# Two-layer diffusion backbone on one core: a matrix cast by its transfer, a later 1/rms, and a new order of the last FFN's operand sums

## The chip, the core and the metric

The kernel runs on one core of a Trainium2 chip. The metric is device time in microseconds. A core has engines that each work through their own queue in order: TensorE (PE) for matmuls, VectorE (DVE), ScalarE (ACT), GpSimd (POOL) and SyncE (SP). SP and POOL mostly start transfers (DMA). An instruction that waits holds up everything behind it on its engine.

## The reference

The reference is a hybrid backbone with two layers over 1024 latent tokens of width 1024 and 256 context tokens.

```
layer 0:  p = u @ w_in;  y = [2-D Fourier mix | order-2 Hyena (short conv, two long convs by FFT)] @ w_out
layer 1:  neighbourhood attention (16 heads, relative bias, all context keys) @ w_out
each:     u = rms_norm(h, norm_g) * (1 + scale) + shift        # scale and shift from the conditioning vector
          h = h + g1 * mixer(u)
          h = h + g2 * ((silu(u2 @ w_gate) * (u2 @ w_up)) @ w_down)
out:      rms_norm(h_lat, final_g)
```

Here `rms_norm(x, g) = x * rsqrt(mean(x * x) + 1e-6) * g`. The FFN has 2816 hidden channels. In layer 1 only the latent tokens go on to the output projection and the FFN.

## The kernel before

Activations are held channel by token: a tile has 128 channels on the partitions and 512 tokens in the free dimension. `pc` 0 and 1 are the two halves of the latent tokens, `pc` 2 the context. Each float32 product is made of three matmuls: an operand is split into a rounded high part (a cast on ACT) and the low part that is left (a subtraction on DVE). `split` at L285 does this for weights and activations (L287 is the cast, L289 the subtraction); `out` in `wino_second` does the same at L1172 and L1173. So an operand is ready only when ACT and then DVE have worked on it. Weights come through `weights` (L307): a float32 load into a `ws` buffer by SP, then the split into `wh` and `wl`. These three tags have two buffers each.

A scheduler decides at build time in which order the instructions stand in each engine's queue. `self.follow(x)` (L226) makes it place what is issued inside behind the instruction x. The generators in the source (their `yield`s are the steps) say what is issued in which order; the scheduler may move instructions where dependences allow.

**First forward transforms (layer 0).** `in_proj` (L744) multiplies 16 blocks of the input projection and feeds `short_conv` (L727; ACT L737, then DVE L738 to L741). Then `hy_forward("l", 0)` (L791) transposes the folded channels on TensorE (L802), splits them (L287, L289), and multiplies them with the matrices `vf_l`. Each matrix comes as float16: `cmat` (L321) loads it through SP into a `cs` tile of the tag `ws` and ACT casts it (L335) into a `mat` tile of the tag `wh` or `wl`. Another helper, `cast` (L338), already used elsewhere for the matrices `ff_l`, starts a transfer on POOL's queue that converts on the way and writes the `mat` tile directly; it goes round the tags `wh`, `wl`, `ws`.

**Last output projection (layer 1).** `first_part(1)` (L2040) multiplies the first six of eight channel blocks of the second token half with `w_out2`: eight blocks of output channels, 18 matmuls each, with a yield behind each three. Behind each block `add_h` (L2030) adds to the residual h2. The loop at L2075 weaves in the RMS norm of the first token half. `square` (L470) has squared its eight blocks on ACT (L475) into tiles of the pool `tk`, which has four buffers, and added them on DVE (L480). At step 2 `rms_begin(0)` (L482) adds over the channels with four matmuls of one column and takes square root and reciprocal (L493, L495). At step 5 `rms_end` (L498) spreads 1/rms over the partitions: four scalings of the identity on ACT (L504) and one matmul. From there `wino_first` (L1148) makes the FFN's operands of the first half, one step at each third step. The attention's last output rows are stored from `tk` tiles as well (`d<-tk` on POOL's queue).

**Last FFN (layer 1).** `ffn` multiplies by a seven-product Winograd scheme over 2 x 2 blocks (token halves by channel halves). `wino_steps` (L1264) orders the products: A11*B11, A12*B21, S1*T1, S2*T2, S3*T3, A22*T4, S4*B22, each over four 128-row pieces j = 0 to 3, for gate and up. The S operands come from weights, the T operands from activations: `wino_second` (L1163) makes T1 (four times: `scaled(j)`, a subtraction, `out`), then T2 (`scaled(j + 4)` at L1179, a sum at L1195, `out`), then T3 (sum at L1200, `out`), T4 (sum at L1206, `out`) and B22. `scaled` multiplies a block of the second half by its norm and modulation. In layer 1 the `scaled(j + 4)` of T2 follow the last subtraction of T1; the sums of T3 and T4 are free to move. `snap` (L1277) copies an accumulator from PSUM on ACT (L1279) before the next product is added to it.

Of the kernel before, what the change touches and what calls it, by code (L numbers as in the profile page):

```python
# [10 lines left out]
F32 = mybir.dt.float32  # L11
# [5 lines left out]
MUL, ADD, SUB, MAX, MIN = ALU.mult, ALU.add, ALU.subtract, ALU.max, ALU.min  # L17

P = 128
# [181 lines left out]
class Builder:  # L201
# [40 lines left out]
    def T(self, dt=F32, w=512):  # L242
        self.tk = (getattr(self, "tk", 0) + 1) % 8
        if self.tk >= 6 and self.banks == 8 and not hasattr(self, "od"):
            return self.TK(dt, w)
        return self.pt.tile([P, w], dt, tag="t", name=self.nm("t"))
# [4 lines left out]
    def PS(self):  # L251
        self.pk = (self.pk + 1) % self.banks
        return self.PQ() if self.pk >= 6 else self.pp.tile([P, 512], F32, tag="ps", name=self.nm("ps"))
# [244 lines left out]
    def rms_end(self, pc, c, copy=True):  # L498

        nc = self.nc  # L500
        w = WID[pc]
        t = self.T()
        for j in range(w // P):
            nc.scalar.mul(t[:, j * P:(j + 1) * P], self.ident, c[:, j:j + 1])  # L504
        ps = self.PS() if self.banks == 8 else self.PQ()
        self.mm(ps[:, :w], self.ones, t[:, :w], True, True)
        if copy:
            nc.scalar.copy(t[:, :w], ps[:, :w])
            return t
        return ps  # L510
# [280 lines left out]
    def hy_forward(self, sq, o):  # L791
        nc, a = self.nc, self.a
        PS, T = (self.PS, self.T) if sq == "l" else (self.PQ, self.T)
        nb = 4 if sq == "l" else 1
        H = nb * P
        ab = self.ab[sq]
        tr = {}
        for b in range(nb):
            for s in (0, 1):
                ps = PS()  # L800
                for cb in range(4):
                    nc.tensor.transpose(ps[:, cb * P:(cb + 1) * P], ab[cb][:, s * H + b * P:s * H + (b + 1) * P],  # L802
                                        self.ident)
                hi, lo = self.S2(F32R), self.S2(F32R)
                self.split(ps, hi, lo)
                tr[(s, b)] = (hi, lo)
        yield
        Y = self.Y[(sq, o)] = {}
        for cls in (0, 1):
            for fb in range(nb):  # L810
                spec = []
                for i, s in ((cls, cls), (2 + cls, 1 - cls)):
                    mt = self.cmat(2 * H, a["vf_" + sq][i, fb], None, False)
                    mh, ml = mt[:, :H], mt[:, H:]
                    ps = PS()
                    for b in range(nb):
                        sl = slice(b * P, (b + 1) * P)
                        xh, xl = tr[(s, b)]
                        self.mm(ps, mh[:, sl], xh, b == 0, False)
                        self.mm(ps, mh[:, sl], xl, False, False)  # L820
                        self.mm(ps, ml[:, sl], xh, False, b == nb - 1)
                    spec.append(ps)
                d = self.frg[(sq, o, cls, fb)]
                fr, g = self.TK(), self.TK()
                self.ld(fr, d[0])
                self.ld(g, d[1])
                fr2 = fr
                if cls == 0 and fb == 0:
                    fr2 = self.S2()
                    self.ld(fr2, d[2])  # L830
                c, s = spec
                for kind, (x0, x1, op) in enumerate((((c, fr), (s, g), SUB), ((c, g), (s, fr2), ADD))):
                    t0, t1 = T(), T()
                    nc.vector.tensor_tensor(t0, x0[0], x0[1], MUL)
                    nc.vector.tensor_tensor(t1, x1[0], x1[1], MUL)
                    nc.gpsimd.tensor_tensor(t0, t0, t1, op)
                    if nb == 4:
                        key = (kind, cls, fb // 2)
                        if key not in Y:
                            Y[key] = (self.S4(F32R), self.S4(F32R))  # L840
                        hi, lo = (q[:, (fb % 2) * 512:(fb % 2) * 512 + 512] for q in Y[key])
                    else:
                        hi, lo = self.S2(F32R), self.S2(F32R)
                        Y[(kind, cls, 0)] = (hi, lo)
                    self.split(t0, hi, lo)
                yield
# [316 lines left out]
    def wino_second(self, h, l, m, r):  # L1163

        nc = self.nc
        dsh = self.C(4)
        ad = self.ada[(l, 0)]
        nc.vector.tensor_tensor(dsh, ad[:, m * 8 + 4:m * 8 + 8], ad[:, m * 8:m * 8 + 4], SUB)

        def out(key, j, src):  # L1170
            hi, lo = self.pair((key, j), l == 1 or len(self.X) < 17)
            nc.scalar.copy(hi, src)  # L1172
            nc.vector.tensor_tensor(lo, src, hi.bitcast(F32), SUB)  # L1173

        ts, sub = [], None

        def scaled(b):
            t = h.ap(0, b, 1)
            nc.vector.scalar_tensor_tensor(t, t, self.ada_col(l, 1, m + 1, b), r, op0=MUL, op1=MUL)  # L1179
            return t  # L1180

        for j in range(4):
            t11, t21 = self.raw.pop(j), self.raw.pop(j + 4)
            with self.follow(sub if l else None):
                t12 = scaled(j)
            sub = nc.vector.tensor_tensor(t11, t12, t11, SUB).ins
            out("T1", j, t11)
            ts.append([t11, t12, None, t21])
            yield
        for j in range(4):  # L1190
            with self.follow(sub if l else None):
                ts[j][2] = t22 = scaled(j + 4)
            t11 = ts[j][0]
            sh = self.ada_col(l, 1, m, j + 4)
            nc.vector.scalar_tensor_tensor(t11, t22, sh, t11, op0=ADD, op1=SUB)  # L1195
            out("T2", j, t11)
            yield
        for j in range(4):
            t11, t12, t22, t21 = ts[j]
            nc.vector.scalar_tensor_tensor(t12, t22, dsh[:, j:j + 1], t12, op0=ADD, op1=SUB)  # L1200
            out("T3", j, t12)
            yield
        for j in range(4):
            t11, t12, t22, t21 = ts[j]
            sh = self.ada_col(l, 1, m, j + 4)
            nc.vector.scalar_tensor_tensor(t21, t21, sh, t11, op0=ADD, op1=SUB)  # L1206
            out("T4", j, t21)
            yield
        for j in range(4):
            t22 = ts[j][2]  # L1210
            sh = self.ada_col(l, 1, m, j + 4)
            hi, lo = self.pair(("B22", j), l == 0 and len(self.X) < 17)
            nc.scalar.activation(hi, t22, AF.Identity, bias=sh)
            nc.vector.scalar_tensor_tensor(lo, t22, sh, hi.bitcast(F32), op0=ADD, op1=SUB)
            yield
# [604 lines left out]
    def run(self):  # L1820
        nc, a = self.nc, self.a
# [195 lines left out]
        h2, o, h4 = Act(), Act(), Act()  # L2017
# [21 lines left out]

        def first_part(pc):  # L2040
            for nb in range(KB):
                wh, wl = self.weights(a["w_out2"][nb, :, :768], 768, load=None if pc else self.ldr)
                acc = self.PQ() if pc == 0 else self.PS()
                for kb in range(6):
                    if pc == 0 and nb == 0:
                        load_o(kb, (0,), self.ld)
                        yield 1
                    if pc == 0 and nb == 2:
                        load_o(kb, (1,), self.ld)
                    if kb == 2:  # L2050
                        if pc or nb == 0:
                            load_h2(nb, pc)
                        if pc == 0 and nb < 7:
                            load_h2(nb + 1, pc)
                    for w, part in ((wh, 0), (wh, 1), (wl, 0)):
                        self.mm(acc, w[:, kb * P:(kb + 1) * P], by_row(o.ap(part, kb, pc)),
                                kb == 0 and w is wh and part == 0, kb == 5 and w is wl)
                    yield 0.5
                add_h(nb, pc, acc)
# [15 lines left out]
        for i, _ in enumerate(first_part(1)):  # L2075
            if i == 2:
                c = self.rms_begin(0)
            if i == 5:
                first = self.wino_first(h2, 1, 3, self.rms_end(0, c))
            if i > 5 and i % 3 == 1:  # L2080
                next(first, None)
        sums = {}
        drain(self.wino_pair(1, 0, 0, sums, self.G))
# [31 lines left out]
        c = self.rms_begin(1)  # L2115
# [85 lines left out]
```

## Time and profile before

| | us |
|---|---|
| median of three runs | 3024.45 (3024.08 to 3025.89) |
| profiled execution, its time | 3021.79 |
| profiled execution, its span | 3020.0 |
| TensorE busy | 2894.4 |
| DVE busy | 2079.7 |
| ACT busy | 1363.0 |
| POOL busy | 478.9 |

The span runs from the first to the last instruction of the profiled execution. A row of a timeline gives the start, the busy time, the engine, the line of the source, the operation, output and inputs by the program's names, and the number of instructions that the row joins; in brackets stands how long the engine was idle before and what ended that. In a table of stretches each engine has its busy time and instructions (in parentheses), and behind them stand the clock granted to TensorE as a share of full speed, the busy share of the DMA engines and the GB/s moved.

### The profile page before, as it was taken

The numbers are of one execution on the slowest core, as the hardware profiler recorded it, in microseconds if no ns is written. First come the engines' busy times: TensorE is split into PE (matmuls) and PEld (weight loads), VectorE is DVE, ScalarE is ACT, GpSimd is POOL, SyncE is SP. The second block draws the span as 40 slices with busy tenths as digits, with TensorE's granted clock in tenths as the row PEclk, the third lists the DMA queues.
The fourth block names the chain that finished last, engine by engine and source line by source line (L and its number), as shares of the span: only waits on it lengthen the run. The fifth ranks groups of instructions, "written<-read, shape, count | busy, mean of one in ns | idle before, by whom it ended". The sixth has DMA issues, their size and how long they took to land. (4 is left out here: it accounts for less than half of the span.)

```text
span 3020.0 us, 45776 instructions
## 1 busy us (share of the span) xinstructions
PE 2894.4 (96%) x16320; PEld 2414.6 (80%) x16320; DVE 2079.7 (69%) x3988; ACT 1363.0 (45%) x2549; POOL 478.9 (16%) x785
## 2 busy tenths in 40 slices
PE   7899999999999999999999999999899999999997
PEld 2678888888899788788888888878777788888886
DVE  5677786675677777876777437777677977665454
ACT  3453325453455333333445337777675533333442
POOL 1112013452100111112020000110111022112000
PEclk9899999999999999999999999999999999999998
DMA  8764545456555554659884344444555266435663
GB/s 279 247 222 168 178 146 172 122 181 230 189 183 196 174 185 170 213 186 324 318 291 155 126 129 118 129 139 124 177 184 203 89 235 216 175 113 184 212 194 119
DMA packets 263486, 558.26 MB, mean 185 GB/s; under 512 B 33878, under 2 KB 85784, under 8 KB 263258
## 3 DMA queue, kind: packets, MB, share of 16 engines
q1 hardware_dynamic: 205050, 372.84, 37.8%
q0 software_dynamic: 55904, 178.30, 16.5%
q10 hardware_dynamic: 2304, 4.20, 0.4%
q8 instruction: 128, 2.10, 0.3%
q14 instruction: 100, 0.82, 0.1%
HBM read 418.63 MB, written 119.80 MB: 178 GB/s over the span
## 5 line engine op out<-in xcount | busy, mean ns | idle before, releaser
L1274 PE MATMUL ps<-s,s 128*128 128x512 f32 x2028 | 505.9, 391 | 12.8 <-ACT g L1279 4.6
L1274 PEld LDWEIGHTS ps<-s,s 128*128 128x128 f32 x2028 | 380.9, 188 | 97.2 <-ACT g L1279 7.1
L283 PE MATMUL ps<-s,wh 128*128 128x256 f32 (+1 forms) x1768 | 393.4, 328 | 2.3 <-DVE s L720 1.2
L283 PEld LDWEIGHTS ps<-s,wh 128*128 128x128 f32 x1768 | 292.7, 189 | 38.1 <-ACT wh L287 2.5
L283 PE MATMUL pq<-s,wh 128*128 128x512 f32 (+1 forms) x984 | 299.4, 383 | 0.6 <-DVE s L1658 0.6
L287 ACT CAST wh<-ws 128x1024 fp32r<-128x1024 f32 (+1 forms) x139 | 142.4, 1024 | 334.7 <-PE ps L283 158.4
L1445 PE MATMUL ps<-s,s 128*128 128x512 f32 (+1 forms) x1000 | 258.4, 383 | 4.5 <-DVE s L289 4.4
L289 DVE TENSOR_TENSOR wl<-ws,wh 128x1024 fp32r<-128x1024 f32 (+1 forms) x139 | 165.3, 1190 | 136.0 <-ACT wh L287 134.2
L283 PE MATMUL ps<-s,wl 128*128 128x256 f32 (+1 forms) x884 | 255.8, 326 | 1.2 <-DVE wl L289 1.2
L287 ACT CAST s<-s 128x1024 fp32r<-128x1024 f32 (+2 forms) x184 | 168.2, 940 | 187.9 <-DMA s<-d 169.6
L283 PE MATMUL ps<-s,s 128*128 128x64 f16 (+3 forms) x2663 | 217.0, 233 | 24.3 <-DVE st L1743 10.3
L287 ACT CAST s<-t 128x512 fp32r<-128x512 f32 (+2 forms) x250 | 139.7, 579 | 182.2 <-DVE t L1253 68.4
L289 DVE TENSOR_TENSOR s<-s,s 128x1024 fp32r<-128x1024 f32 (+2 forms) x162 | 186.8, 1184 | 46.9 <-ACT s L287 46.4
L1445 PEld LDWEIGHTS ps<-s,s 128*128 128x128 f32 x1000 | 184.4, 188 | 42.9 <-DVE s L289 6.7
L289 DVE TENSOR_TENSOR s<-t,s 128x512 fp32r<-128x512 f32 (+2 forms) x250 | 166.9, 680 | 57.8 <-ACT s L287 31.2
L283 PEld LDWEIGHTS pq<-s,wh 128*128 128x128 f32 x984 | 177.7, 190 | 34.2 <-DVE s L1658 2.1
L1274 PE MATMUL ps<-s,wh 128*128 128x512 f32 x608 | 193.3, 395 | 0.3 <-DVE g L1367 0.3
L283 PE MATMUL ps<-s,mat 128*128 128x512 f32 x684 | 178.5, 408 | 4.9 <-ACT s L287 4.0
L283 PE MATMUL pq<-s,wl 128*128 128x512 f32 (+1 forms) x492 | 182.1, 380 | 0.0
L283 PEld LDWEIGHTS ps<-s,wl 128*128 128x128 f32 x884 | 162.6, 188 | 18.4 <-DVE wl L289 1.9
L283 PEld LDWEIGHTS ps<-s,mat 128*128 128x128 f32 x684 | 132.3, 196 | 39.8 <-ACT s L287 6.2
L1445 PE MATMUL ps<-s 128*128 128x512 f32 (+1 forms) x500 | 149.4, 385 | 0.0
(381 smaller groups left out, 5621.8 us busy)
## 6 DMA issues: line engine op xcount, KB each, us to landing
s<-d SPq DMA_DIRECT2D x282, 256.0 KB, 3.6
s<-in_down SPq DMA_DIRECT2D x150, 256.0 KB, 4.0
d<-s POOLq DMA_DIRECT2D x137, 256.0 KB, 3.6
d<-tk POOLq DMA_DIRECT2D x98, 256.0 KB, 3.6
s<-in_ada_w POOLq DMA_DIRECT2D x48, 512.0 KB, 4.7
g<-in_bias SPq DMA_DIRECT2D x128, 192.0 KB, 2.8
ws<-in_up SPq DMA_DIRECT2D x44, 512.0 KB, 3.4
d<-g POOLq DMA_DIRECT2D x87, 256.0 KB, 3.1
```

The lines of the kernel that those rows point to most:

```text
L283: self.nc.tensor.matmul(o, l, r, start=st, stop=sp)
L287: self.last_hi = nc.scalar.copy(hi, src).ins
L289: self.last_lo = eng.tensor_tensor(lo, src, hi.bitcast(F32), SUB).ins
L1274: nc.tensor.matmul(ps, x[:, sl], y, start=first and j == 0 and x is wh and y is xh, stop=j == 3 and x is wl, skip_group_check=True)
L1445: m = nc.tensor.matmul(acc[j][:, c0:c1], x[:, sl], y[:, xs], start=first and k == 0, stop=last and k == 2, skip_group_check=True)
```

## The change

There are three edits.

1. The first four `vf_l` matrices of the first forward transform (`cls` 0, `fb` 0 and 1, two each) are fetched with `cast` instead of `cmat`.
2. `rms_end(0)` and `wino_first` are issued at step 11 of `first_part(1)` instead of step 5, and `wino_first` advances from step 13 on. The loads and splits of that projection's weights for blocks 3 to 8 (`nb` over 1) follow the last scaling of the most recent `rms_end`, which is the one of step 11 for those blocks.
3. In layer 1, `wino_second` notes every low-part subtraction of `out`. The scalings `scaled(j + 4)` follow the third one (T1, j = 2), the sums of T3 follow the seventh (T2, j = 2), and the sums of T4 follow the eleventh (T3, j = 2). The scalings no longer follow the last subtraction of T1.

```
@@ rms_end
-            nc.scalar.mul(t[:, j * P:(j + 1) * P], self.ident, c[:, j:j + 1])
+            self.last_mul = nc.scalar.mul(t[:, j * P:(j + 1) * P], self.ident, c[:, j:j + 1]).ins
@@ hy_forward
-                    mt = self.cmat(2 * H, a["vf_" + sq][i, fb], None, False)
+                    src = a["vf_" + sq][i, fb]
+                    mt = self.cast(2 * H, src) if sq == "l" and o + cls == 0 and fb < 2 else self.cmat(2 * H, src)
@@ wino_second
-            nc.vector.tensor_tensor(lo, src, hi.bitcast(F32), SUB)
+            los.append(nc.vector.tensor_tensor(lo, src, hi.bitcast(F32), SUB).ins)
+
+        los = []
+
+        def behind(n):
+
+            return self.follow(los[n] if l else None)
...
-            with self.follow(sub if l else None):
+            with behind(2):
                 ts[j][2] = t22 = scaled(j + 4)
...
-            nc.vector.scalar_tensor_tensor(t12, t22, dsh[:, j:j + 1], t12, op0=ADD, op1=SUB)
+            with behind(6):
+                nc.vector.scalar_tensor_tensor(t12, t22, dsh[:, j:j + 1], t12, op0=ADD, op1=SUB)
...
-            nc.vector.scalar_tensor_tensor(t21, t21, sh, t11, op0=ADD, op1=SUB)
+            with behind(10):
+                nc.vector.scalar_tensor_tensor(t21, t21, sh, t11, op0=ADD, op1=SUB)
@@ first_part
-                wh, wl = self.weights(a["w_out2"][nb, :, :768], 768, load=None if pc else self.ldr)
+                with self.follow(self.last_mul if pc and nb > 1 else None):
+                    wh, wl = self.weights(a["w_out2"][nb, :, :768], 768, load=None if pc else self.ldr)
@@ the loop over first_part(1)
-            if i == 5:
+            if i == 11:
                 first = self.wino_first(h2, 1, 3, self.rms_end(0, c))
-            if i > 5 and i % 3 == 1:
+            if i > 11 and i % 3 == 1:
                 next(first, None)
```

## The prediction

> **What bounds the kernel now.** I read the page's busy shares first, then the idle gaps of TensorE, then for each gap the queue that ends it, and last the granted clock around the gaps. Line numbers are those of the kernel before.
>
> ```profile
> span 3020.0 us, 45776 instructions
> ...
> PE 2894.4 (96%) x16320; PEld 2414.6 (80%) x16320; DVE 2079.7 (69%) x3988; ACT 1363.0 (45%) x2549; POOL 478.9 (16%) x785
> ...
> core 0: 3020.0 us, clock 0.989
> ```
>
> TensorE is busy for 2894.4 of 3020.0 us, so all that scheduling could win in the whole kernel is 125.6 us plus what a low clock costs. The change takes no matmul away. It can pay only at the gaps it touches. The timeline of TensorE shows three of them (last bracket: idle before the row and what ended it):
>
> ```profile
> 455.91 1.91 PE L802 MATMUL ps<-c,s 128*128 128x128 f32 x16
> 461.19 2.08 PE L802 MATMUL ps<-c,s 128*128 128x128 f32 x16 [3.37 <-DVE s L289]
> ...
> 2310.57 2.07 PE L283 MATMUL ps<-t,c 128*128 128x512 f32 x2 [4.98 <-ACT t L504]
> ...
> 2375.31 0.73 PE L1274 MATMUL pq<-s,s 128*128 128x512 f32 x2 [0.90 <-DVE s L1173]
> ...
> 2381.81 8.94 PE L1274 MATMUL ps<-s,s 128*128 128x512 f32 x32 [4.33 <-DVE s L1173]
> 2391.66 5.98 PE L1274 MATMUL ps<-s,s 128*128 128x512 f32 x25 [0.90 <-ACT g L1279]
> ```
>
> They hold 3.37, 4.98 and 0.90 + 4.33 + 0.90 = 6.13 us. The stretches below give the clock after each gap (first number after the five busy times); the last two rows are matmuls of the timeline, six apart:
>
> ```profile
> 2309.90:2316.50 6.60, 5.93 (x12) 4.03 (x13) 5.03 (x8) 4.24 (x9) 0.00 (x0) 0.50 0.10 41
> 2381.60:2384.80 3.20, 2.99 (x7) 2.41 (x8) 3.20 (x6) 3.20 (x7) 0.00 (x0) 0.50 0.00 0
> 456.34:459.75 3.41, 1.48 (x14) 1.24 (x12) 2.46 (x5) 3.41 (x7) 0.58 (x2) 1.00 1.09 263
> 541.67:545.08 3.41, 1.76 (x11) 1.21 (x10) 1.79 (x13) 1.13 (x5) 0.00 (x0) 1.00 0.61 184
> 545.20:551.80 6.60, 6.35 (x28) 5.95 (x28) 3.69 (x18) 1.16 (x5) 1.46 (x3) 0.50 0.36 102
> 2292.03:2296.24 4.21, 4.21 (x20) 3.40 (x18) 2.76 (x5) 2.30 (x4) 1.50 (x3) 1.00 0.89 306
> 2304.64:2334.19 29.55, 24.57 (x96) 19.13 (x95) 23.75 (x36) 15.89 (x25) 0.00 (x0) 0.88 0.32 109
> ...
> 2313.30 0.63 PE L283 MATMUL ps<-s,wl 128*128 128x512 f32 x1
> ...
> 2315.86 0.63 PE L283 MATMUL ps<-s,wl 128*128 128x512 f32 x1
> ```
>
> The clock is 0.50 for some 6.6 us behind the second gap and some 3.2 us behind the third; behind the first it stays 1.00. A block of 18 matmuls takes 4.21 us at full clock, 0.234 each; at the low one they are 2.56 / 6 = 0.427 apart, so 45% of the time is lost there. The five blocks from 2304.64 on need 21.05 of that stretch's 29.55 us. The other 8.50 us are the 4.98 us stall and 3.52 us of low clock and five small matmuls.
>
> **Edit 1, matrices cast by their transfer.** It removes four SP transfers and four ACT casts, and adds four casting transfers on POOL's queue. The matmuls and their order stay. Timelines of ACT, TensorE, DVE and POOL, and the rows of a matrix that is already fetched in this way:
>
> ```profile
> 455.52 1.05 ACT L335 CAST mat<-cs 128x1024 fp32r<-128x1024 f16 x1 [10.19 <-DVE c L456]
> 456.48 0.77 ACT L737 ACTIVATE s<-ps,c 128x512 f32<-128x512 f32 x1
> ...
> 458.26 1.04 ACT L335 CAST mat<-cs 128x1024 fp32r<-128x1024 f16 x1
> ...
> 463.02 9.31 PE L283 MATMUL ps<-s,mat 128*128 128x512 f32 x39
> ...
> 457.29 0.75 DVE L738 SCALAR_TENSOR_TENSOR s<-ps,c,s 128x511 f32<-128x511 f32 x1 [1.57 <-ACT s L737]
> ...
> 451.87 1.11 POOL L274 DMA_DIRECT2D s<-in_cg_c  x2 [5.17 <-DVE ah L454]
> ...
> L274 POOL DMA_DIRECT2D mat<-in_ff_l x32: 527/527/557, 17.4 to 182.5; - x32
> ...
> DMA to landing us min/median/max: 3.3/3.6/11.6
> ```
>
> Two of the casts lie far from the gap. The one at 455.52 stands directly ahead of the first short-convolution operation at 456.48, which starts DVE's run of work up to the gap's end at 461.19. Without it ACT can start when the last projection matmuls end, near 456.0: 0.5 us earlier. The cast at 458.26 does not go: the fifth matrix, still cast by ACT, takes its place. So the gap shrinks from 3.37 to about 2.9. Bounds: nothing, if the matmuls end later than I read them, and 1.0 us, the length of the cast. The SP time saved is hidden by queued loads. On POOL's queue the fourth matrix must wait for its buffer, free after the projection at about 455.7, and the eight context loads that start at 451.87 wait behind it. They move by about 4 us; a later stage reads them. The matrix lands at 455.7 + 0.5 + 3.6 = 460, or at 468 by the longest row; it is used behind the 36 matmuls of three matrices that start at 463.02, at 463.0 + 36 x 0.234 = 471.4. Cost nothing, with 3 us of cover left at worst; each microsecond beyond is one of TensorE. Term: -0.5.
>
> **Edit 2, 1/rms six steps later.** Six steps are one block of `first_part(1)`. In the built order the four matmuls that add up the squares (`rms_begin`) move too: before they stand behind the third block, now directly behind the first, which ends at 2296.24. Are the sums ready there?
>
> ```profile
> 2295.31 2.19 ACT L475 ACTIVATE tk<-s 128x512 f32<-128x512 f32 x4 [1.91 <-DMA d<-tk]
> ...
> 2290.80 1.17 POOL L274 DMA_DIRECT2D d<-tk  x2
> ...
> DMA to landing us min/median/max: 4.3/4.4/4.5
> ...
> 2295.97 1.49 DVE L480 TENSOR_TENSOR tk<-tk,tk 128x512 f32<-128x512 f32 x2 [1.45 <-ACT tk L475]
> ...
> 2298.64 0.95 DVE L289 TENSOR_TENSOR wl<-ws,wh 128x768 fp32r<-128x768 f32 x1
> 2299.51 1.48 DVE L480 TENSOR_TENSOR tk<-tk,tk 128x512 f32<-128x512 f32 x2
> ...
> 2307.44 1.28 ACT L493 ACT_TABLE_LOAD   x1
> ...
> 2309.24 1.28 ACT L504 ACTIVATE t<-c,st 128x128 f32<-128x128 f32 x4 [0.24 <-DVE st L495]
> ```
>
> No. Four of the eight squares wait for two attention stores, issued from 2290.80 on, which land 4.3 to 4.5 us later, because they want the buffers these leave. After that come five dependent adds, about 0.8 us each, and one residual add: from 2295.97 they end at 2301.0 today, and at 2300.3 once the weight split at 2298.64 (0.95, of which 0.6 to 0.9 counts) has gone behind the 1/rms. So TensorE, in order, stalls from 2296.24 to 2300.3: 4.06 us. What vanishes is the stall of 4.98. Behind block 2 the 1/rms matmul then finds its input: table load 1.28, root and reciprocal 0.5, four scalings 1.3, from 2300.8 to about 2304, while block 2 runs until 2305. The splits for blocks 3 to 8 follow from there; DVE has 0.3 us to spare at the tightest, and if that is gone TensorE waits that much. One load of the residual moves ahead of POOL's queue, into a buffer long free: nothing.
>
> The clock goes low behind this stall too, as it lies across a whole idle stretch like the old one. If for 6.6 us as there, 4.06 + 3.52 = 7.6 replaces 8.5: -0.9. If for 3.2 us as after the third gap, 3.4 us less at 45% lost cost 1.5 us less: -2.4. The two rows differ and neither is nearer; I take -1.5. Bounds -0.9 and -2.4, with +0.5 if stores land a microsecond or so later.
>
> The Trainium skill ("TensorE: Matmul & The Clock Gate", Part 1) describes a free-running window of about 3.4 us: idle throughout, the clock halves; busy for one, it returns. By that rule the low stretch is one window, the term is -2.4 and the time 3019.3. The trace agrees at 2381.60 and not at 2309.90, where it lasted twice as long with TensorE busy 5.93 of 6.60 us.
>
> **Edit 3, order of T2, T3, T4.** Same DVE and ACT instructions, new order. DVE is the queue that runs without a hole here:
>
> ```profile
> 2370.05 2.74 DVE L1179 SCALAR_TENSOR_TENSOR s<-s,c,t 128x512 f32<-128x512 f32 x4
> 2372.70 0.68 DVE L1173 TENSOR_TENSOR s<-s,s 128x512 fp32r<-128x512 f32 x1
> ...
> 2376.49 2.07 DVE L1200 SCALAR_TENSOR_TENSOR s<-s,c,s 128x512 f32<-128x512 f32 x3
> ...
> 2381.07 0.69 DVE L1173 TENSOR_TENSOR s<-s,s 128x512 fp32r<-128x512 f32 x1
> ...
> 2386.07 4.29 DVE L1173 TENSOR_TENSOR s<-s,s 128x512 fp32r<-128x512 f32 x7
> ...
> 2370.42 1.14 ACT L1172 CAST s<-s 128x512 fp32r<-128x512 f32 x2
> ```
>
> Ahead of T2's first low part at 2381.07, the one TensorE waits for, four T3 sums and one T4 sum (L1200, L1206; 0.66 us each) now go behind it: 3.3 us. Against that, T1's third low part moves ahead of the four scalings and waits for ACT's cast at 2370.42 (DVE idle 1.0 us), and two T2 sums that stood behind the first low parts come ahead. Counting through the new order at 0.60 to 0.66 us each, T2's first low part ends at 2380.1 instead of 2381.76. TensorE restarts 1.7 us earlier. If the clock goes low as before, the 18 matmuls end at 2385.7. T2's last low part (2384.6), T3's first three (by 2386.4) and fourth (2389.7), and the low part of the up product S1 (2390.3; its ten matmuls now stand behind T3's) each come before TensorE gets there, by 0.05 to 1 us. The copy that released 2391.66 stands earlier on ACT, and its gap falls from 0.90 to about 0.5. T4's product starts at 2395.0 instead of 2397.25. Term: -2.2. Bounds: -0.7 with a low stretch twice as long, -3.6 with none (3.06 us at 45%, 1.4).
>
> **Sum.** -0.5 - 1.5 - 2.2 = -4.2 us, so 3017.6 for the profiled execution's 3021.79. That execution is 2.66 below the median of the three runs, 3024.45; on the median it gives 3020.2. Adding the bounds: -7.0 to -0.2, or 3017.4 to 3024.2. About 0.2% (6 us) is what a measurement of this kernel can tell from no change.
>
> **The rivals.**
>
> The sums come early: with the weight splits away, the two stores land 4 us sooner and nothing stalls behind block 1. Edit 2 gives 8.5 less 0.8 for the small matmuls, 7.7; total -10.4: 3014.0. For it: DMA share 0.89 in that stretch, which a later weight load could relieve. Against: the stores are issued at 2290.80, ahead of any load that moves.
>
> The clock stays full behind both stalls: edit 2 gives 8.5 - 0.8 - 4.06 = 3.6, edit 3 3.6, edit 1 0.5: 3016.8. For it: the stretch at 456.34 was busy only 1.48 of 3.41 us and kept its clock. Against: the stalls of 4.06 and 3 us each.
>
> The stalls only change place: DVE's spare of 0.05 to 0.3 us is gone in both parts, and each gain turns into a new wait: 3024.4.
>
> Slower, by the clock alone: everything behind 460 us moves by half a microsecond and behind 2300 by several, so half-busy stretches are cut elsewhere. The stretch at 541.67 was busy 1.76 us and was followed by 6.6 us at 0.50, while the less busy one at 456.34 was not. One more such drop costs 45% of 6.6, 3.0 us. Two make +1.8: 3026.2; from four on the kernel is slower by more than 0.2%, 3032.2. Against it: equally many drops can vanish.
>
> **How the numbers follow.** Forecast (3017.4 to 3024.2 as its own range) 0.42; sums early 0.18; clock full 0.12; stalls change place 0.10; slower by the clock 0.18, 0.13 of it beyond 0.2%. Faster by over 0.2%: 0.18 + 0.12 + 0.03 of the forecast's edge = 0.33; slower 0.13; within 0.2% 0.54. The range 3012.5 to 3027.5 holds all but the worse of the clock's cases and an early sum with a full clock.
>
> **What would show it.** Edit 1: the gap before the second sixteen transposes near 2.9 us, no casts of these four matrices. Edit 2: four matmuls of one column behind block 1, with some 4 us idle ahead of them released by a DVE add, then no idle before the 1/rms matmul. Edit 3: the gap before T2's matmuls near 3 us, T4's product 2.2 us earlier relative to the wait's start. It is wrong if the squares do not wait for the stores, if the casting transfers land late, or if mean clock (0.989 today) moves by over 0.002.

## The result, and the profile after

The changed kernel takes 3013.93 us (median of six runs, 3012.68 to 3016.80); the kernel before, run beside it, takes 3025.17 (3023.28 to 3029.29). The ratio is 0.9959 with a 95% interval of 0.9948 to 0.9970: 11.2 us faster, between 9.1 and 15.7. A second comparison in another session gave 3010.94 against 3021.21, 0.9966 (0.9955 to 0.9978). The profiled execution took 3012.68 us. From its page:

```profile
span 3010.8 us, 45798 instructions
...
PE 2890.9 (96%) x16320; PEld 2414.9 (80%) x16320; DVE 2075.4 (69%) x3988; ACT 1359.2 (45%) x2545; POOL 479.1 (16%) x789
```

The number of matmuls is the same, yet TensorE's busy time fell by 3.5 us, from 2894.4. Keep that in mind: idle gaps cannot explain it. The clock can explain part of it, since the stretches at half clock sum to 47.8 us in this profile and to 54.1 in that of the kernel before.

The three places, in the timeline of TensorE of the changed kernel (last bracket: idle before the row, and what ended it; in this kernel L1274 has become L1283, L1173 is L1174 and L1279 is L1288):

```profile
457.97 1.91 PE L802 MATMUL ps<-c,s 128*128 128x128 f32 x16
462.66 2.08 PE L802 MATMUL ps<-c,s 128*128 128x128 f32 x16 [2.77 <-DVE s L289]
...
2298.56 1.86 PE L283 MATMUL ps<-c,tk 128*128 128x1 f32 x8 [3.50 <-DVE tk L480]
...
2306.26 1.02 PE L283 MATMUL pq<-t,c 128*128 128x512 f32 x2
...
2372.45 0.73 PE L1283 MATMUL pq<-s,s 128*128 128x512 f32 x2 [1.68 <-DVE s L1174]
2373.76 1.25 PE L1283 MATMUL ps<-s,s 128*128 128x512 f32 x4 [0.58 <-ACT s L1173]
2376.90 5.65 PE L1283 MATMUL ps<-s,s 128*128 128x512 f32 x22 [1.89 <-DVE s L1174]
2384.30 13.45 PE L1283 MATMUL ps<-s,s 128*128 128x512 f32 x58 [1.75 <-ACT g L1288]
```

The first gap is 2.77 us instead of 3.37. The column sums of the squares stand behind one block and wait 3.50 us for a DVE add of the squares; the 1/rms matmul at 2306.26 waits for nothing. T2's product starts after gaps of 1.68, 0.58 and 1.89, and the copy ends a gap of 1.75.

To weigh the places against the scatter, I cut TensorE's records of every profile at the same matmuls and took the time of each stretch. Fourteen profiles are at hand: the two of the kernel before and of the changed one, and ten experiments of the next section (one profile of each).

| stretch | without the edit there (us) | with it (us) | mean difference |
|---|---|---|---|
| gap of edit 1 alone | 3.36 to 3.37 (8 profiles) | 2.77 to 2.78 (6) | -0.6 |
| 54 us around the column sums (edit 2) | 55.62 to 56.48 (9) | 54.39 to 55.11 (4) | -1.2 |
| 65 us around T2 (edit 3) | 64.71 to 65.77 (9) | 62.84 to 64.07 (5) | -1.8 |
| last feed-forward layer behind it, 575 us | 574.66 to 575.68 (7: those without edit 1, but for e23 with 577.2, of which more below) | 574.11 and 574.83 (changed kernel) | -0.7 |
| last 32 us, by edit 1 | 31.72 to 33.58 (8) | 29.88 to 30.93 (6) | -1.9 |
| first to last matmul | 2993.8 to 3004.0, mean 2997.7 (5: twice the kernel before, and pool4, sp4, before_mj, which leave the three places alone) | 2989.7 and 2987.3 (changed kernel) | -9.2 |

The three places hold 3.6 us, near the 4.2 that was forecast. The result is some 6 us more. The experiments looked for it.

### The profile page after: what moved, and what is told of

It reads as the page before. It is cut to its first block, busy times and chain, and to the rows that moved or that the text cites. A ratio compares the mean times of both kernels' runs of the same rounds, so it can differ in the third digit from the quotient of the medians.

```text
span 3010.8 us, 45798 instructions
## 1 busy us (share of the span) xinstructions
PE 2890.9 (96%) x16320; PEld 2414.9 (80%) x16320; DVE 2075.4 (69%) x3988; ACT 1359.2 (45%) x2545; POOL 479.1 (16%) x789
## 5 line engine op out<-in xcount | busy, mean ns | idle before, releaser
L1283 PE MATMUL ps<-s,s 128*128 128x512 f32 x2028 | 503.6, 390 | 9.2 <-ACT g L1288 3.5
L1283 PEld LDWEIGHTS ps<-s,s 128*128 128x128 f32 x2028 | 379.6, 188 | 93.8 <-ACT g L1288 6.4
L1283 PE MATMUL ps<-s,wh 128*128 128x512 f32 x608 | 192.2, 393 | 0.0
```

The costliest lines, as they stand in the source:

```text
L1283: nc.tensor.matmul(ps, x[:, sl], y, start=first and j == 0 and x is wh and y is xh, stop=j == 3 and x is wl, skip_group_check=True)
```

## The experiments

Ratios are against the kernel before, run on the same chip in the same session; its medians were 3029.23, 3021.21 and 3020.64 us in the three sessions.

**Each edit alone.** The theory on record, that the three terms add up, against rivals in which one edit carries all.

`e1_alone`, edit 1 only:
```diff
-                    mt = self.cmat(2 * H, a["vf_" + sq][i, fb], None, False)
+                    src = a["vf_" + sq][i, fb]
+                    mt = self.cast(2 * H, src) if sq == "l" and o + cls == 0 and fb < 2 else self.cmat(2 * H, src)
```


> Edit 1 alone: four forward matrices cast by their transfer, the rest as before. Theory (sum of the three places): the gap ahead of the second sixteen transposes shrinks from 3.37 to about 2.8 us and the kernel gains 0.6 us, which the timing cannot tell from nothing. Rival (the part of the gain that the three places do not hold, some 5 to 7 us, comes from edit 1's transfers and casts off the queues): 4 us or more faster.

`e2_alone`, edit 2 only:
```diff
...
+                with self.follow(self.last_mul if pc and nb > 1 else None):
+                    wh, wl = self.weights(a["w_out2"][nb, :, :768], 768, load=None if pc else self.ldr)
...
-            if i == 5:
+            if i == 11:
...
-            if i > 5 and i % 3 == 1:
+            if i > 11 and i % 3 == 1:
```


> Edit 2 alone: 1/rms six steps later, weights of blocks 3 to 8 behind it. Theory: first_part(1) gets 1.7 us shorter as in the changed kernel (stall ahead of the column sums 3.5 us, low clock behind it), and nothing else changes: -1.7 us. Rival: the gap of 1.72 us before 2766.70 and the shorter end of the kernel also belong to edit 2 (another order of what follows): 5 us or more faster, with no gap near 2765.

`e3_alone`, edit 3 only:
```diff
...
-            with self.follow(sub if l else None):
+            with behind(2):
...
+            with behind(6):
+                nc.vector.scalar_tensor_tensor(t12, t22, dsh[:, j:j + 1], t12, op0=ADD, op1=SUB)
...
+            with behind(10):
+                nc.vector.scalar_tensor_tensor(t21, t21, sh, t11, op0=ADD, op1=SUB)
```


> Edit 3 alone: order of T2, T3, T4. Theory: 1.9 us at the T2 to T4 products as in the changed kernel, and the order it sets for the following products removes the gap of 1.72 us before 2766.70: -2 to -4 us together. Rival: only the place of the edit gains, the gap near 2766 stays: -1.9 us; and if the clock goes low behind the T1 and T2 stalls here, only -0.5 us.

Measured: e1_alone 3018.47 us, 0.9969 (0.9958 to 0.9979), that is -9.4 us (-12.7 to -6.4); e2_alone 3024.85, 0.9984 (0.9972 to 0.9995), -4.9; e3_alone 3025.66, 0.9986 (0.9975 to 0.9997), -4.2. These differences are the ratio's share of 3029.23 us. The intervals of edits 2 and 3 begin at -1.5 and -0.9 us: the stretch of edit 3 (-1.8) lies within, that of edit 2 (-1.2) just outside. The gap near 2766 that both expectations speak of stays in both, with 1.06 and 1.51 us, so the second half of the theory for e3_alone fell. Edit 1, the one forecast to be the smallest, gives most, and far more than its gap. The three add up to 18.5 us, more than the 10 to 11 us of the whole change in the other sessions. All three are judged by the same runs of the kernel before, so an error of that median would count three times; whether that is the reason is open.

**Both late edits together.** `e23`, edits 2 and 3 without edit 1 (both diffs above).

> Edits 2 and 3 without edit 1. Sum of the places: -1.4 and -1.9, that is -3.3 us (-1.7 to -5 with scatter). If the gap of 1.7 us in the second half of the last feed-forward layer (before the 64 matmuls at 2766.7) is taken by edits 2 and 3 together, that stretch is 217.4 to 218.2 us instead of 218.7 to 219.4, and the sum is -4.5; if it needs edit 1 as well, it stays. The last stretch stays at 31.7 to 32.9 us if that gain is edit 1's alone.

Measured: 3018.05, 0.9992 (0.9982 to 1.0002), -2.4 us (-5.5 to +0.6). The gap of 1.72 us at 2766.7 is gone, as in the first profile of the changed kernel (its second keeps 0.49 us there, and in the other profiles of the kernel before and its like the gap is 0.7 to 1.5). But the gain isn't there: the two stretches of the last layer take 359.66 + 217.57 = 577.2 us, against 574.7 to 575.7 before. One row of the timeline of before and two of e23:

```profile
2768.42 3.02 PE L1274 MATMUL ps<-s,s 128*128 128x512 f32 x12 [1.72 <-ACT g L1279]
```

```profile
2411.02 11.23 PE L1282 MATMUL ps<-s,s 128*128 128x512 f32 x48 [0.67 <-ACT s L287]
...
2769.30 3.03 PE L1282 MATMUL ps<-s,s 128*128 128x512 f32 x12
```

The wait moved from the layer's middle to its first weights, where before had no idle at all and e23 has 2.07 us in several gaps, of which the row shows one: a stall that only changes place. In the changed kernel this about cancels (the last layer gains no more than e1_alone's 574.2 already has), so nothing of the 6 us lies there.

**What of edit 1 ends the kernel sooner?** In the last 32 us one gap is 1.83 us before and 0.57 after. Timeline of TensorE, of before and of the changed kernel:

```profile
2986.95 1.22 PE L1445 MATMUL ps<-s,s 128*128 128x256 f32 x8 [1.83 <-DVE s L289]
```

```profile
2979.02 1.22 PE L1454 MATMUL ps<-s,s 128*128 128x256 f32 x8 [0.57 <-DVE s L289]
```

The stores of the output in the view of their tile, of before (the first row is who waited for them: us, times) and of the changed kernel:

```profile
  DVE g L2094: 1.2, 1
...
DMA to landing us min/median/max: 2.1/2.5/3.9
```

```profile
DMA to landing us min/median/max: 2.1/2.5/2.7
```

Before, a DVE operation waits 1.2 us for a store to leave its buffer, and the slowest store takes 3.9 us to land; in the changed kernel it takes 2.7. Edit 1 moves four transfers from SP's queue to POOL's, 2500 us earlier. Two theories: what counts is the stores' place on POOL's queue, or the length of SP's.

`pool4` (the kernel before and four casting transfers more on POOL's queue) and `sp4` (four transfers more on SP's), both into a buffer that nothing reads:
```diff
...
+                    if sq == "l" and o + cls == 0 and fb < 2:
+                        with self.follow(self.last_sub):
+                            self.ldr(self.DR([P, 2 * H + 32])[:, :2 * H], src)
...
+                    if sq == "l" and o + cls == 0 and fb < 2:
+                        with self.follow(self.last_ld):
+                            self.ld(self.dr.tile([P, 2 * H + 32], F16, name=self.nm("d"), tag=self.nm("dt"))[:, :2 * H], src)
```


> The kernel before, with four more casting transfers of the same shape on POOL's queue at the place of edit 1, from the same matrices into scratch memory that nothing reads. SP's transfers and ACT's casts stay. It separates what edit 1 takes off ACT and SP from what it adds to POOL's queue. Theory (edit 1's gain of some 9 us outside its place comes from POOL's later transfers standing at another place of their queue): the first four output stores land after 2.6 us instead of 3.8 to 4.4, the end of the kernel is 2 us shorter, and the whole is 5 us or more faster although more is done. Rival (the gain comes from the relief of ACT and SP): no faster, or slower by up to 3 us, with the stores as late as before.

> The kernel before, with four more transfers of the same matrices on SP's queue, without a cast, into scratch memory that nothing reads, spread over the same place. Theory (SP's queue is not what edit 1 gained from): no difference that the timing can tell, output stores at 3.8 to 4.4 us. Rival (the number of SP's transfers, which edit 1 lowers by four, matters for what comes later): 3 us or more of difference, either way.

`e1_sp4`: edit 1, and sp4's four transfers beside it.

> Edit 1 alone, with four transfers of the same matrices left on SP's queue as well, into a buffer that nothing reads (work is added, none left out), so that every later SP transfer has the place in the queue that it has in the kernel before. If the shorter SP queue is what makes the last stores land sooner and the last stretch shorter: 31.7 to 32.9 us there and a time of -0.6 to -6 us. If not: 29.9 to 30.9 us there, and -6 to -12 us.

Measured: pool4 3020.48, 0.9997 (0.9985 to 1.0009), last stretch 32.00 us; sp4 3021.62, 1.0006 (0.9997 to 1.0016), 32.05; e1_sp4 3016.27, 0.9977 (0.9966 to 0.9989), 30.92. Both theories fall: neither queue's length brings the shorter end or takes it away. What does so stays open.

**The buffers.** Edit 1 also deals its matrices to other buffers. The first guess was the counter that deals cast matrices over three rings: `e1_mj` sets it back behind the four, `before_mj` sets it forward in the kernel before.
```diff
...
+                    if early and (fb, i) == (1, 2 + cls):
+                        self.mj = (self.mj - 4) % 3
...
+                    if sq == "l" and o + cls == 0 and fb < 2:
+                        self.mj = (self.mj + 1) % 3
```


> Edit 1 alone, but behind the four casting transfers the counter that deals later cast matrices over three buffers is set back, so that all later matrices lie in the buffers of the kernel before. Edit 1 alone gave -9.4 us (about -12.7 to -6.4), of which its own gap holds 0.6 and the last stretch (from the last transposes on) 1.3 to 2. If the other buffers of the later matrices are the cause, most of it goes: -0.6 to -3 us, and the last stretch is back at 31.7 to 32.9 us. If they are not: -6 to -12 us again, and the last stretch at 29.9 to 30.9 us. The gap before the second sixteen transposes is 2.8 us in both cases.

> The kernel before with nothing changed but that counter: the later cast matrices lie in the buffers that edit 1 gives them, and the first matrices come as before. If the buffers are the cause of what edit 1 gives beyond its place: -4 to -9 us and a last stretch of 29.9 to 30.9 us. If not: within 3 us of the kernel before, with 31.7 to 32.9 us there. The gap stays 3.4 us.

Measured: e1_mj 3013.57, 0.9976 (0.9965 to 0.9986), -7.1 us; before_mj 3020.94, 1.0001 (0.9990 to 1.0011). These say nothing on the guess, because it was badly made: no cast matrix comes after those four, so the counter is not used again. They are repeats of edit 1 alone and of the kernel before, and as such useful: edit 1 is worth about 7 us on this chip too.

`before_again` and `after_again` are repeats by intent.

> The kernel before, a second profile. Theory (its first profile, 3021.79 us, was taken at a lucky phase of the clock, since it lies below nearly all other runs): 3025 to 3031 us, with more low clock than the 54 us of the first, and the output stores at 3.8 us or more again. Rival (the profile was typical): 3021 to 3024 us with the same low clock.

> The changed kernel again, beside the runs of the kernel before that the single edits are judged by. Theory (the gains of the edits add up, and edit 1 has most of it): 11 to 15 us faster, with low clock in other places than in the first profile, and the stall of 3.5 us ahead of the column sums, the 1.9 us gap ahead of T2 and no gap near 2765 again. Rival (the edits get in each other's way): less than 8 us faster.

Measured: before_again 3016.69 us in a single run, after_again 3010.94 (3010.24 to 3011.74), 0.9966, that is -10.3 us. Neither the theory nor the rival for before_again came true: it has more low clock than the first profile (61.1 us against 54.1) and is faster all the same, in another session. after_again lies between its theory and its rival; the stall ahead of the column sums is there again (3.68 us), and so are 0.49 us near 2765.

**Where edit 1's gain is.** The repeats made a pattern visible in the profiles. Take a stretch of the last layer in which TensorE is never idle and the clock is full, 2400 to 2750 us: before, and then e1_alone (first number after the stretch's length: TensorE's busy time and its matmuls):

```profile
2400.00:2750.00 350.00, 350.00 (x1534) 288.16 (x1533) 239.31 (x364) 125.58 (x206) 59.06 (x110) 1.00 0.50 175
```

```profile
2400.00:2750.00 350.00, 350.00 (x1539) 288.70 (x1538) 238.74 (x364) 124.18 (x204) 63.37 (x118) 1.00 0.50 175
```

Both are 100% busy, but five more matmuls went through: each takes less time. By groups of operands in that stretch (mean ns of one, last number before the zero), before and then e1_alone:

```profile
L1274 PE MATMUL ps<-s,s 128*128 128x512 f32 x755 | 188.6, 389 | 0.0
L1274 PE MATMUL ps<-s,wh 128*128 128x512 f32 x208 | 66.1, 394 | 0.0
...
L1274 PE MATMUL ps<-s,wl 128*128 128x512 f32 x104 | 41.2, 397 | 0.0
```

```profile
L1275 PE MATMUL ps<-s,s 128*128 128x512 f32 x747 | 187.1, 389 | 0.0
L1275 PE MATMUL ps<-s,wh 128*128 128x512 f32 x208 | 65.6, 392 | 0.0
...
L1275 PE MATMUL ps<-s,wl 128*128 128x512 f32 x104 | 40.7, 392 | 0.0
```

Only the matmuls that read weights (`wh`, `wl`) changed. The built programs tell in which buffers these lie. Each ring has two, 4224 bytes per partition apart, which is 16.5 times 256: the first of each begins at a multiple of 256 bytes, the second 128 beyond one. I sorted all float32r matmuls of 512 columns, where start to next start is 216 to 250 ns, by the start addresses of their two operands and of the next matmul's:

```
                                     before            e1_alone
all at a multiple of 256       5505 at 227.3 ns   6355 at 227.4 ns
one or more 128 beyond it      2902 at 233.5 ns   2071 at 234.2 ns
weights with wh and wl in like buffers      2                 162
weights with wh and wl in unlike buffers  176                  16
```

The same matmuls can be compared with each other too, since three profiles with edit 1 alone and the five of the kernel before and its like issue them in the same order. Of those in the table's range of 216 to 250 ns in all eight (ns from start to next start, means):

```
addresses, before to edit 1 alone          matmuls   before   edit 1 alone
128 beyond, then all at a multiple             990    233.0          228.2
all at a multiple, then 128 beyond             131    228.9          233.4
all at a multiple in both                     5332    227.3          227.2
128 beyond in both                            1882    233.8          234.3
```

A matmul whose buffers change class changes its time, in both directions; one that keeps its class keeps its time within 0.5 ns. The change shows in one timeline as well. Of the changed kernel, weights that lie in two first buffers, and 15 us later weights in two second buffers (first and last row of each piece):

```profile
2426.15 0.39 PE L1283 MATMUL ps<-s,wl 128*128 128x512 f32 x1
...
2430.46 0.39 PE L1283 MATMUL ps<-s,wl 128*128 128x512 f32 x1
```

```profile
2441.57 0.64 PE L1283 MATMUL pq<-s,wh 128*128 128x512 f32 x2
...
2447.16 0.62 PE L1283 MATMUL ps<-s,s 128*128 128x512 f32 x2
```

19 matmuls in 4.31 us are 226.8 ns each; 24 in 5.59 us are 232.9. So a matmul costs 5 to 6 ns more when it, or the weight load for the one behind it, reads from a second buffer. The code takes two products with the high part and one with the low part in turn. With both parts in first buffers no step of that round is slow, with both in second buffers all three; if they are mixed, 5 of 6 are slow on average, since each change between them counts. Before, nearly all weights were mixed. Edit 1 takes three matrices instead of four from the rings of the parts (one of its four goes to the staging ring), so from there on the two rings run in step, and a third of the weight matmuls gets fast.

On the 8916 matmuls that run undisturbed in all fourteen profiles, the time from start to next start sums to 2047.9 to 2048.2 us in the eight without edit 1 and to 2044.0 to 2044.6 in the six with it. This is 3.8 us, and no profile lies between. No kernel that changes only the buffers, without the edit, was run. The comparison of the same matmuls ties the time to the buffer; that it is the remainder by 256, and not something else that goes with the buffer, is read from the traces and not tried.

**Sums two blocks later.** The stall ahead of the column sums was foreseen as the price of edit 2's form. `late_sums` is the changed kernel with the four one-column matmuls issued one more pair of blocks later, and block 3's matmuls held behind them:
```diff
...
-            if i == 2:
+            if i == 8:
...
+                self.sums_mm = self.last_mm
-            if i == 11:
+            if i == 17:
...
+                    with self.follow(self.sums_mm if pc and nb == 2 else None):
```


> The changed kernel with rms_begin issued at step 8 and placed ahead of block 3, and rms_end at step 17, with the weights of blocks 4 to 8 behind it. Theory (the sums of squares are ready only some 3.5 us after block 1, as they wait for the attention's stores): the stall of 3.50 us ahead of the column sums goes and with it the half clock of 6.8 us behind it, so first_part(1) loses another 5 to 6 us: 5 us faster than the changed kernel, some 16 us faster than the kernel before. Rival (the stall follows the move, because the stores or the adds also come later, or block 4 waits for its weights): no faster than the changed kernel.

Measured: 3007.01 us (3004.57 to 3008.24), 0.9923 (0.9911 to 0.9935), as the theory said and with more than its 16 us. Timeline of TensorE and the stretch around it:

```profile
2299.42 1.05 PE L283 MATMUL ps<-c,tk 128*128 128x1 f32 x8
...
2304.60 1.02 PE L283 MATMUL pq<-t,c 128*128 128x512 f32 x2
```

```profile
2286.00:2334.00 48.00, 48.00 (x210) 38.15 (x209) 42.93 (x62) 27.29 (x43) 9.66 (x18) 1.00 0.64 228
```

Neither the sums nor the 1/rms wait, the clock stays full, and the stretch that took 56.0 before and 54.8 with edit 2 takes 48.37. This is the fastest version, 22 us under the kernel before in its session; that session's runs of the kernel before were the slowest of the three and the changed kernel was not among them, so how much of it would be seen elsewhere is not known beyond the 6.4 us of this stretch.

## Why the prediction was right or wrong

The time, 3013.93, lies in the range and below the forecast's own range of 3017.4 to 3024.2; the forecast of "within 0.2%" as the likeliest was wrong. Of 11.2 us the terms gave 4.2. The wide range held the time by luck: its lower part stood there for rivals whose mechanisms did not bring the gain.

**Edit 1's gap: right.** -0.5 forecast, -0.6 measured, in six profiles of six. The late casting transfers cost nothing, as argued: they land after 3.5 to 4.6 us, and TensorE runs without idle for 37 us behind that gap.

**Edit 1's other cost: this step failed.** "The matmuls and their order stay" was true, and it was taken to mean that their time stays. The step left out that a tile that is no longer dealt from a ring moves every later tile of that ring to the other buffer. It is worth 3.8 us from 460 us to the end. The last 32 us add 1.0 in edit 1 alone (30.92 against 31.97, the mean of the kernel before and its like), whose cause is not settled. Together 0.6 + 3.8 + 1.0 = 5.4 us. From first to last matmul the three profiles with edit 1 alone take 2989.7, 2992.5 and 2995.2 us, on average 5.2 less than the kernel before and its like, so in the profiles little is left over. The timed runs give more: the 5.4 us are within the intervals of the repeat (from 4.2 on) and of e1_sp4 (from 3.3), and short of the 6.4 us from which that of the first run goes on. Some of that rest may be half-clock stretches: the gap at 460 us was followed by one in six of eight profiles without edit 1 and in three of six with it, and each costs 1.5 us. That is too few to tell.

**Edit 2: right in its mechanism, and the size within 0.3, in part by luck.** The sums wait behind block 1 for the squares (3.50 us here, 3.6 to 4.05 in the other profiles with this stall, forecast 4.06), and the 1/rms matmul then waits for nothing. -1.5 forecast, -1.2 measured. The -1.5 stood midway between two cases, and the one with the long low clock came, whose term was -0.9, with a somewhat shorter stall. The low clock lasted twice 3.41 us again. Both halves of that stretch in the changed kernel, then both halves of it in the kernel before and the low stretch of T2 there (first number after the length: TensorE's busy time):

```profile
2297.15:2300.56 3.41, 2.00 (x9) 2.00 (x10) 1.25 (x2) 0.57 (x2) 0.94 (x2) 0.50 0.99 347
2300.57:2303.98 3.41, 3.41 (x9) 2.64 (x9) 3.19 (x6) 2.64 (x7) 0.00 (x0) 0.50 0.40 163
```

```profile
2309.76:2313.17 3.41, 2.60 (x4) 1.47 (x5) 1.94 (x4) 1.86 (x5) 0.00 (x0) 0.50 0.23 92
2313.17:2316.58 3.41, 3.41 (x9) 2.64 (x9) 3.28 (x5) 2.59 (x5) 0.00 (x0) 0.50 0.00 0
2381.46:2384.87 3.41, 3.06 (x7) 2.48 (x8) 3.41 (x7) 3.41 (x8) 0.00 (x0) 0.50 0.00 0
```

The Trainium skill ("TensorE: Matmul & The Clock Gate", Part 1) gives one busy window of some 3.4 us for the clock's return. These rows agree with it, against the prediction's reading of 2309.90: the low stretch comes in steps of 3.41 us, and where it has two, the first still holds the end of the stall (busy 2.00 and 2.60 of 3.41 us) and the second is busy throughout. How busy is enough is not shown: 3.06 of 3.41 us was, and in after_again 3.18 was not, of which 1.87 went to the one-column matmuls. The term of -2.4 was too large because it took one such step for the whole low stretch.

**Edit 3: right in sum, wrong in one part.** -2.2 forecast, -1.8 measured. T2 starts 1.69 us earlier than before, measured from the same matmul ahead of T1's last gaps, where 1.7 was counted, and that in all five profiles with edit 3. But "the copy that released 2391.66 stands earlier on ACT, and its gap falls to about 0.5" failed: it is 1.75. ACT's timeline of the changed kernel shows why:

```profile
2378.75 2.61 ACT L1173 CAST s<-s 128x512 fp32r<-128x512 f32 x4 [2.45 <-DVE s L1208]
2382.55 0.62 ACT L287 CAST s<-t 128x512 fp32r<-128x512 f32 x1 [1.19 <-DVE s L1174]
...
2383.67 0.58 ACT L1288 COPY g<-ps 128x512 f32<-128x512 f32 x1
```

The copy stands behind casts that wait 2.45 us for a sum of T3, which edit 3 put later, and 1.19 us for a low part. The gap also hangs on the clock, as a slower TensorE comes later to the copy. In this profile no low clock came, where a low stretch was forecast. e23 has none either and a gap of 1.13 us; e3_alone has 3.4 us of low clock and 1.15; after_again and late_sums have 6.8 us and 0.21 and 0.22.

**The rivals.** The time came nearest to "the sums come early" (3014.0), but its mechanism did not occur: the sums waited. "Clock full behind both stalls" holds for one of the two, T2's, in two profiles (the first of the changed kernel and e23). "Stalls only change place" did happen, at a fourth place, the last layer of e23. "Slower by the clock alone" was the wrong sign, but its premise is true: the total of half-clock stretches in the fourteen profiles is 48 to 70 us, with 54 to 61 in the five of the kernel before and its like.

**The sum.** 0.6 + 1.2 + 1.8 at the three places, 3.8 by the rate of the weight matmuls and 1.9 in the last 32 us (31.97 for the kernel before and its like against 30.07 for the changed kernel's two profiles) are 9.3 us, of which some 0.2 is counted twice, as the rate acts in the three stretches too. TensorE's first to last matmul says 9.2, the medians 11.2 and 10.3, with intervals from 9.1 and 6.7 on. In the prediction's own sum, the smallest gains that it names for the three terms (0, 0.9 less 0.5, and 0.7) add up to 1.1 us and not to the 0.2 that it gives as the lower bound.

## What to carry to other kernels

An edit that takes a tile out of a ring of two buffers changes the address of everything dealt from that ring afterwards; so compare the time per matmul, by operand, in a stretch without idle, before looking for lost waits. A stall that is moved should go to where other matmuls cover it: late_sums won 6 us more than edit 2 in that way. Measure each edit alone, the one with the smallest term too: here it held about half.

## What the runs showed of the hardware

- A matmul of 512 columns that reads an operand 128 bytes beyond a multiple of 256, or stands ahead of one that does, takes about 233.5 ns from start to start, and 227.3 where all begin at a multiple of 256. The changed kernel has about as many slow ones as e1_alone, 2051 and 2058 in its two profiles. Buffers of 4352 bytes instead of 4224 would put the ring's at multiples of 256; from these rows that is an estimate of 2071 x 6.8 ns = 14 us at most, or 10 us with the 4.8 ns that the 990 matmuls gained, and it wasn't tried.
- The clock was low for 6.83 us around the ends of the stalls of 4.98 us before and 3.50 after, and for 3.41 at T2 before: whole steps of 3.41 us, the last of them with TensorE busy for 3.41, 3.41 and 3.06 us. In e3_alone, behind a stall of 5.38 us, it was low for 10.24.
- The same program runs with other half-clock stretches each time: two profiles of the kernel before have 54.1 and 61.1 us of them, two of the changed one 47.8 and 59.2. Runs of the kernel before spread over 12 to 15 us in a session.
- The slowest of the stores at the end took 3.4 to 4.4 us to land without edit 1 (8 profiles) and 2.7 to 3.1 with it (6), whatever the number of transfers on either queue.
